# A two-layer diffusion backbone: summing the first MLP's second product in DRAM instead of in SBUF

## The chip, the cores and the metric

The kernel runs on one core of one Trainium2 chip. The metric is the device time of one execution in microseconds, and the number compared is the median of several runs. Three runs of the kernel before gave 1179.66, 1181.38 and 1181.9 us.

The engines are named as the profile names them: PE is TensorE (PEld its weight loads), DVE is VectorE, ACT is ScalarE, POOL is GpSimd and SP is SyncE, which in this kernel issues the transfers. PSUM is the memory into which matmuls accumulate, SBUF the working memory, DRAM the memory outside the core.

## What is computed

512 latent tokens and 256 context tokens, each a row of 1024 float32 numbers, go through two layers. Each layer mixes tokens (layer 0 by multi-scale pooling, layer 1 by attention) and then applies an MLP with a squared ReLU; every sub-layer is wrapped in RMS norms with shift, scale and gate from a conditioning vector. The part that matters here is the MLP of layer 0, which works on all 768 tokens:

```python
def sq_relu_mlp(h, w_in, w_out):                # h (768, 1024), w_in (1024, 4096), w_out (4096, 1024)
    return jnp.square(jax.nn.relu(h @ w_in)) @ w_out
...
m_lat = sq_relu_mlp(modulate(rms_norm(x, g_mlp_pre[i]), sh2, sc2), w_mlp_in[i], w_mlp_out[i])
x = x + gt2 * rms_norm(m_lat, g_mlp_post[i])
```

The second product, with w_out, is a sum over 4096 hidden columns. The kernel takes these in 16 groups of 256, so that the 768 x 1024 result is a sum over 16 groups.

## The kernel before, in words

**Numbers and tiles.** Every float32 operand of a matmul is split into a high and a low part (an ACT copy makes the high part, a DVE subtraction the low part), and a product is three matmuls: high x high, high x low, low x high. The 768 tokens are NT = 6 tiles of 128 rows. `acc` is a buffer of SBUF, [128, 6 x 1024] float32 (24 KB in each partition), and `accv[:, t]` is its tile t: 512 KB over the 128 partitions.

**The group loop** (`mlp0`, lines 798 to 824). For g = 0 to 14, one turn computes the hidden columns of group g + 1 (the "inner" product), and for g = 0 to 13 it also adds the second product of group g. For g = 0 the inner product is straightforward (class `Inner`); from g = 1 on it is done as seven smaller products by sums and differences of operands (class `Seven`, line 677), 12 matmuls each, 84 in all. After the fifth product DVE adds two results (lines 693 and 695) that the seventh product and the ReLU wait for. The second product (`out_mm`, line 757) takes, for each of the six tiles, two PSUM buffers of 128 x 512 from the pool `psB` (four buffers, shared with other uses) and 12 matmuls (line 773): 72 matmuls per group.

**Where the sum is kept.** `out_ev` (line 777) moves each PSUM buffer into `accv[:, t]`. In group 0 it copies (line 781, on ACT or DVE). In later groups there are two ways. The usual one is a DVE addition, acc = acc + PSUM (line 785). For tiles 1 and 4, in groups that `stale` doesn't exclude, the kernel "seeds": ACT first copies acc into the PSUM buffer (line 765), the matmuls accumulate onto it (start is false), and ACT copies the sum back (line 783). The last two groups, 14 and 15, are done together by `finish` (line 787) in tile order 4, 5, 0, 1, 2, 3: 24 matmuls per tile, then a DVE addition onto acc, and the norm and residual of that tile follow.

**Weights.** Per turn SP loads 1 MB of w_mlp_out, 1 MB of w_mlp_in and, until the list runs out, two pieces of 1 MB of w_ada, into the pool `rawp`, which has three buffers: a load can be issued when the buffer of three loads earlier has been read for the last time. The weights of w_mlp_out are split by ACT (line 126) and DVE (line 129). Those of w_mlp_in go through `weights_sums` (lines 635 to 665), with ACT casts at 643 and 659 and DVE operations at 644, 651 to 656 and 660. The pieces of w_ada are for `ada_sum` (lines 257 to 273), in which DVE multiplies and adds eight blocks (lines 263 and 268), transposes (271) and reduces (272). POOL has no work in this loop; it computes small row statistics (lines 161 to 169) elsewhere.

**What sets the order.** The kernel is written with a tile framework whose scheduler orders the instructions of each engine ahead of time, by its own model of durations, and places the semaphore waits; each engine then runs its list in order. In some places a list of due times (`Steps`) or a pinned order steers it. A transfer waits on the engine that issues it. `spill` is a tensor in DRAM that holds the residual rows (xr) during the MLP; they are read back (line 1158) ahead of the finish.

Of the kernel before, what the change touches and what calls it, by code (L numbers as in the profile page):

```python
# [9 lines left out]
F32 = mybir.dt.float32  # L10
# [3 lines left out]
ALU = mybir.AluOpType  # L14
# [3 lines left out]
P = 128  # L18
D = 1024
# [5 lines left out]
NT = TOK // P  # L25
# [28 lines left out]
def backbone(ctx: ExitStack, tc, x, c, ctx_in, c_ctx, w_ada, b_ada, g_mix_pre, g_mix_post,  # L54
# [3 lines left out]
    sy, ve, sc, gp, te = nc.sync, nc.vector, nc.scalar, nc.gpsimd, nc.tensor  # L58
# [14 lines left out]
    xr, gate, junk = residents(held[0])  # L73
    psA = ctx.enter_context(tc.tile_pool(name="psA", bufs=2, space=PSUM))
    psB = ctx.enter_context(tc.tile_pool(name="psB", bufs=4, space=PSUM))
    spill = ctx.enter_context(tc.tile_pool(name="spill", bufs=1, space=bass.MemoryType.DRAM)).tile([P, NT, D], F32, name="spill")

    acc = const.tile([P, NT * D], F32, name="acc")
    ident = const.tile([P, P], F32, name="ident")
    cols = const.tile([P, 128], F32, name="cols")  # L80
# [22 lines left out]
    accv = acc.rearrange("p (t n) -> p t n", n=D)  # L103
# [107 lines left out]
    ve.tensor_copy(cols, pp[:, 0:128])  # L211
    ve.tensor_copy(gpc, pp[:, 128:160])

    rowsd, parts, seeded, stale = {}, {}, {}, [0]

    def ada_mm(i, m, j, w=2):
        src = w_ada[i, :, m * D + j * 256: m * D + j * 256 + w * P].rearrange("(k p) n -> p k n", p=P)
# [23 lines left out]
    def ada_out(i, m, j, ps, nc_, w=2):  # L241
        at = m * KT + 2 * j
        ve.tensor_tensor(out=mods[i][:, at:at + w, 0:nc_], in0=ps.rearrange("p (b c) -> p b c", c=nc_),
                         in1=cols[:, i * 48 + at: i * 48 + at + w].unsqueeze(2).broadcast_to([P, w, nc_]),
                         op=ALU.add)
        if (i, m) == (0, SH1):
            ve.tensor_scalar(out=minus[:, 2 * j:2 * j + w], in0=mods[i][:, at:at + w, 0:nc_], scalar1=-1.0,
                             scalar2=None, op0=ALU.mult)
        if m in (SC1, SC2):
            s = 0 if m == SC1 else 1  # L250
            g0 = 96 + s * 16 + i * KT + 2 * j
            ve.scalar_tensor_tensor(out=avec[i][s][:, 2 * j:2 * j + w, 0:nc_], in0=mods[i][:, at:at + w, 0:nc_],
                                    scalar=1.0,
                                    in1=cols[:, g0:g0 + w].unsqueeze(2).broadcast_to([P, w, nc_]),
                                    op0=ALU.add, op1=ALU.mult)
# [19 lines left out]
    def ada_fin(i, m, parts, nc_):  # L275
        n = 4 * nc_
        ps = psB.tile([P, 512], F32, tag="b", name="psada")
        stale[0] = 4
        for a in range(4):
            te.matmul(ps[32 * a:32 * a + 32, 0:2 * n], sel,  # L280
                      parts.rearrange("p (u c b a) -> p a u b c", c=nc_, b=2, a=4)[:, a], start=True, stop=True)
        ada_out(i, m, 0, ps[:, 0:2 * n], nc_, 8)
# [314 lines left out]
    def spill_rows():  # L597
        for t in range(NT):
            tc.keep_in_program_order(sy.dma_start(spill[:, t], xr[:, t]))

    def sums():
        held[0].close()
        S["held"] = ExitStack()
        pool = S["held"].enter_context(tc.tile_pool(name="sums", bufs=1, side="right"))
        f, parts[0] = pool.tile([P, 8520], F32R, name="sums"), pool.tile([P, 192], F32, name="parts")
        u = unit[0]
        n4 = 4 * HN
        at = {1: (f[:, 0:n4], f[:, n4:2 * n4]), 2: (f[:, 2 * n4:3 * n4], f[:, 3 * n4:4 * n4]),
              4: (u[:, 0:n4], u[:, n4:2 * n4])}
        k4 = lambda z: [z[:, HN * k:HN * k + HN] for k in range(z.shape[-1] // HN)]  # L610
        for n, (hi, lo) in at.items():
            S[n] = k4(hi), k4(lo)
        h3, l3 = f[:, 4 * n4:5 * n4], [u[:, 2 * n4:2 * n4 + 2 * HN], f[:, 5 * n4:5 * n4 + 2 * HN]]
        S[3] = k4(h3), [z for x in l3 for z in k4(x)]
        src = acc.rearrange("p (q h u k n) -> p u h k q n", u=2, k=4, h=2, n=P)

        def put(n, j, a, b, op):
            hs = slice(2 * HN * j, 2 * HN * j + 2 * HN)
            wide = lambda z: z.rearrange("p (k q n) -> p k q n", k=2, n=P)
            w = work_tile()[:, 0:2 * HN]  # L620
            for m in range(2):
                ve.tensor_tensor(out=wide(w)[:, m], in0=a[:, m], in1=b[:, m], op=op)
            hi, lo = (h3[:, hs], l3[j]) if n == 3 else (z[:, hs] for z in at[n])
            sc.copy(hi, w)
            ve.tensor_tensor(out=lo, in0=w, in1=hi, op=ALU.subtract)
            return wide(w)

        for j in range(2):
            a11, a21, a12, a22 = (src[:, u, h, 2 * j:2 * j + 2] for u in range(2) for h in range(2))
            w1 = put(1, j, a21, a22, ALU.add)  # L630
            w2 = put(2, j, w1, a11, ALU.subtract)
            put(4, j, a12, w2, ALU.subtract)
            put(3, j, a11, a21, ALU.subtract)
# [73 lines left out]
    def w_in(i, g, rg, pin=False, wait=None):  # L707
        return rg.load(w_mlp_in[i, :, g * 256:(g + 1) * 256].rearrange("(k p) n -> p k n", p=P), 256, pin, wait)

    def w_out(i, g, rg, pin=False):  # L710
        return rg.load(w_mlp_out[i, g * 256:(g + 1) * 256, :].rearrange("(k p) n -> p k n", p=P), D, pin)
# [23 lines left out]
    order = (4, 5, 0, 1, 2, 3)  # L735
# [21 lines left out]
    def out_mm(i, parts, t, cols=HALVES):  # L757
        at_ = place_of[t] if i == 0 else t
        ts_ = slice(at_ * P, (at_ + 1) * P)
        seeded[t] = i == 0 and parts[0][0] > 0 and len(parts) == 1 and t in (1, 4) and stale[0] <= 0  # L760
        stale[0] -= 2
        pss = [psB.tile([P, 512], F32, tag="b", name="pso") for _ in cols]
        if seeded[t]:
            for (c0, w), ps in zip(cols, pss):
                sc.copy(ps, accv[:, t, c0:c0 + w])
        seq = [(a, f, w) for (_, (hi, lo), (wH, wL)) in parts for f in range(2)
               for a, w in ((hi, wH), (hi, wL), (lo, wH))]
        order = [(n, h) for n in range(len(seq)) for h in range(len(cols))]
        if len(parts) > 1:
            order.sort(key=lambda z: (z[0] >= (9 if cols == HALVES else 0), z[1]))  # L770
        for n, h in order:
            a, f, w = seq[n]
            te.matmul(pss[h][:, 0:cols[h][1]], a[:, f, ts_], w[:, f, cols[h][0]:sum(cols[h])],  # L773
                      start=(n == 0 and not seeded[t]), stop=(n == len(seq) - 1), skip_group_check=seeded[t])
        pso[t] = pss

    def out_ev(i, parts, t, cols=HALVES):
        for (c0, w), ps in zip(cols, pso[t]):
            d = accv[:, t, c0:c0 + w]
            if parts[0][0] == 0:  # L780
                (ve.tensor_copy if c0 and t % 3 else sc.copy)(d, ps)
            elif seeded[t]:
                sc.copy(d, ps)  # L783
            else:
                ve.tensor_tensor(out=d, in0=d, in1=ps[:, 0:w], op=ALU.add)  # L785

    def finish(i, parts, order, last, also=()):
        st = Steps()
        for z in also:
            st.at(*z)  # L790
        for n, t in enumerate(order):
            cols = THIRDS if (i, t) == (1, NL - 1) else HALVES
            st.at(5.2 * n, out_mm, i, parts, t, cols)
            st.at(5.2 * n + 5.2, out_ev, i, parts, t, cols)
            last(st, n, t)
        st.run()

    def mlp0(inner, hids, order, extra, mid, last, before_last):
        aH, aL = inner.a
        one = lambda z: Ring([z], True)  # L800
        wi = w_in(0, 1, one(unit[1]), True)
        spill_rows()
        for f in range(2):
            inner.square(f)
        wo_ = w_out(0, 0, one(unit[2]))
        sums()
        for g in range(NG - 1):
            if g:
                wo_, products = w_out(0, g, one(unit[2])), weights_sums(g + 1)
            part = (g, inner.hid, wo_)  # L810
            extra(g)
            if g:
                inner = Seven(products, hids[(g + 1) % len(hids)])
            else:
                inner = Inner(g + 1, wi, aH, aL, hids[(g + 1) % len(hids)], chunks0, TOK)
            inner.run((lambda: mid(g)) if g < NG - 2 else None)
            if g == NG - 2:
                wo_ = w_out(0, NG - 1, one(unit[1]))
            else:
                for t in range(NT):  # L820
                    out_mm(0, [part], t)
                    out_ev(0, [part], t)
        before_last()
        finish(0, [part, (NG - 1, inner.hid, wo_)], order, last)

# [504 lines left out]
    def last1(st, n, t):  # L1330
# [3 lines left out]
        st.at(5.2 * n + 7.8, fin_b, t)  # L1334

    mlp0(first[0], hids0, (4, 5, 0, 1, 2, 3), extra0, mid0, last0, before0)
    mlp1(first1[0], last1)

# [53 lines left out]
```

## Time and profile before

| | |
|---|---|
| median of three runs | 1181.38 us |
| runs | 1179.66 to 1181.9 us |
| span of the profiled execution, first to last instruction | 1177.7 us |
| median of the runs less that span | 3.7 us |
| moved by DMA | 147.84 MB, mean 126 GB/s |
| SP's queue (q1), share of 16 DMA engines over the span | 36.6% |
| mean granted TensorE clock | 0.994 |

The profiled execution's time is known by its span alone; a run's time holds about 3.7 us more than that. In the rows of the profile, "L773" is line 773 of the kernel before; `out<-in` names the tiles written and read; "x1152" is a count; the numbers after it are busy time in microseconds and the mean duration of one instruction in nanoseconds, then the idle time of the engine ahead of these instructions and what ended it. A row of a table of stretches gives the stretch, its length, and the busy time of each engine with its number of instructions. A row of transfers gives the count, the size of one and the median time from issue to landing in microseconds.

### The profile page before, as it was taken

What the parts mean: (1) busy time and instruction counts of PE and PEld (TensorE: products, weight loads), DVE (VectorE), ACT (ScalarE), POOL (GpSimd) and SP (SyncE); (2) the same over time, 40 slices, a digit from 0 to 9 for tenths busy, and PEclk for the clock granted to TensorE, in tenths of its full rate; (3) what the DMA queues carried; (4) which work ended last, traced back from release to release, by engine and by line L of the source; (5) the groups of instructions that cost most, each with busy time, mean ns of one, the idle gap of its engine ahead of it and who ended that gap; (6) DMA issues with size and microseconds to landing.
All of it is one profiled execution on the core that took longest, in us unless ns stands there. A gap on an engine that the chain in (4) does not pass through costs nothing.

```text
span 1177.7 us, 15984 instructions
## 1 busy us (share of the span) xinstructions
PE 1142.0 (97%) x6170; PEld 988.8 (84%) x6170; DVE 941.6 (80%) x1546; ACT 638.0 (54%) x1087; POOL 67.4 (6%) x120
## 2 busy tenths in 40 slices
PE   5899999999999999999999999999899999999997
PEld 4579888989889988998887889998888888888886
DVE  3786778998988999896787689887686779778876
ACT  3766654555354445555676377862676446435522
POOL 2030000000000000000141210001100000000001
PEclk9899999999999999999999999999999999999999
DMA  9994223444444344344422100115334124314312
GB/s 335 353 310 183 72 72 107 143 143 144 143 143 143 116 136 143 107 133 153 180 72 77 68 1 36 37 42 186 122 116 162 67 94 143 107 36 144 107 39 104
DMA packets 100010, 147.84 MB, mean 126 GB/s; under 512 B 2736, under 2 KB 75872, under 8 KB 99936
## 3 DMA queue, kind: packets, MB, share of 16 engines
q1 hardware_dynamic: 99936, 146.84, 36.6%
q8 instruction: 48, 0.79, 0.3%
q14 instruction: 26, 0.21, 0.1%
HBM read 139.49 MB, written 7.34 MB: 125 GB/s over the span
## 4 chain that ended last, share of the span: by engine, by line
PE 52%; issue 33%; DVE 6%; ACT 4%; POOL 3%; DMA 2%; SPq 0%; POOLq 0%; DVEq 0%; ACTq 0%
PE pso L773 22%; PE psin L677 18%; PE psin L553 3%; PE po L1234 2%; PE psq L1020 2%; PE pss L1195 2%; POOL rs L169 1%; PE psada L225 1%; PE psm L420 1%; POOL rs L1029 1%; ACT junk L154 1%; DVE sm L1199 1%; PE pspt L1220 1%; DVE rows L268 1%; DVE units L1223 1%
## 5 line engine op out<-in xcount | busy, mean ns | idle before, releaser
L773 PE MATMUL pso<-units,rb 128*128 128x512 f32 x1152 | 278.9, 392 | 0.0
L773 PEld LDWEIGHTS pso<-units,rb 128*128 128x128 f32 x1152 | 214.7, 188 | 41.1
L268 DVE SCALAR_TENSOR_TENSOR rows<-raw,cond,rows 128x256 f32<-128x256 f32 x280 | 127.3, 480 | 2.0
L785 DVE TENSOR_TENSOR acc<-acc,pso 128x512 f32<-128x512 f32 x129 | 85.4, 677 | 39.4 <-PE pso L773 39.3
L553 PE MATMUL psin<-ra,rb 128*128 128x512 f32 (+1 forms) x432 | 104.8, 342 | 2.4 <-ACT ra L363 1.6
L877 PE MATMUL pso<-units,pairs 128*128 128x512 f32 x336 | 82.3, 389 | 0.0
L553 PEld LDWEIGHTS psin<-ra,rb 128*128 128x128 f32 x432 | 70.3, 189 | 13.6 <-ACT ra L363 1.9
L553 PE MATMUL psin<-ra 128*128 128x512 f32 x256 | 80.4, 389 | 0.0
L877 PEld LDWEIGHTS pso<-units,pairs 128*128 128x128 f32 x336 | 63.1, 188 | 13.1
L881 DVE TENSOR_TENSOR acc<-acc,pso 128x512 f32<-128x512 f32 x72 | 48.7, 683 | 26.4 <-PE pso L877 26.4
L167 POOL TENSOR_SCALAR ms<-ss 128x1 f32<-128x1 f32 x20 | 9.6, 482 | 1000.2 <-ACT junk L154 988.4
L677 PE MATMUL psin<-ra,units 128*128 128x384 f32 x336 | 65.5, 337 | 0.4 <-ACT psin L689 0.4
L677 PE MATMUL psin<-sums,units 128*128 128x384 f32 x336 | 64.0, 336 | 0.0
L677 PEld LDWEIGHTS psin<-ra,units 128*128 128x128 f32 x336 | 59.8, 188 | 3.9 <-ACT psin L689 0.5
L129 DVE TENSOR_TENSOR units<-raw,units 128x1024 fp32r<-128x1024 f32 (+2 forms) x49 | 55.2, 1154 | 6.5 <-ACT units L126 6.3
L677 PEld LDWEIGHTS psin<-sums,units 128*128 128x128 f32 x336 | 58.9, 188 | 1.6
L126 ACT CAST units<-raw 128x1024 fp32r<-128x1024 f32 (+2 forms) x49 | 46.9, 995 | 17.7 <-PE pso L773 13.7
L553 PEld LDWEIGHTS psin<-ra 128*128 128x128 f32 x256 | 48.1, 188 | 10.0
L553 PE MATMUL psin<-rb 128*128 128x512 f32 (+1 forms) x144 | 52.8, 367 | 0.2 <-DVE rb L364 0.2
L1020 PE MATMUL psq<-units,ra 128*128 128x512 f32 x216 | 51.7, 392 | 0.0
L783 ACT COPY acc<-pso 128x512 f32<-128x512 f32 x48 | 27.1, 586 | 43.6 <-PE pso L773 42.9
L553 PE MATMUL psin<-rb,ra 128*128 128x512 f32 x128 | 49.8, 389 | 0.0
(255 smaller groups left out, 2356.0 us busy)
## 6 DMA issues: line engine op xcount, KB each, us to landing
raw<-in_w_ada SPq DMA_DIRECT2D x48, 1024.0 KB, 5.4
raw<-in_w_mlp_in SPq DMA_DIRECT2D x32, 1024.0 KB, 5.4
raw<-in_w_mlp_out SPq DMA_DIRECT2D x32, 1024.0 KB, 5.1
raw<-in_w_qkv SPq DMA_DIRECT2D x6, 1024.0 KB, 5.2
spill<-xr SPq DMA_DIRECT2D x10, 512.0 KB, 9.1
xr<-spill SPq DMA_DIRECT2D x10, 512.0 KB, 6.6
raw<-in_w_o SPq DMA_DIRECT2D x4, 1024.0 KB, 4.9
xr<-in_x SPq DMA_DIRECT2D x4, 512.0 KB, 4.2
```

The lines of the kernel that those rows point to most:

```text
L126: a = sc.copy(hi, raw)
L129: b = ve.tensor_tensor(out=lo, in0=raw, in1=hi, op=ALU.subtract)
L268: ve.scalar_tensor_tensor(out=r, in0=raw[:, k, :], scalar=cond[:, k, c:c + 1], in1=r, op0=ALU.mult, op1=ALU.add)
L553: te.matmul(ps[:, bank, o:o + ln], w[:, k, fs], rhs, start=start, stop=(k == KT - 1 and n == 2), skip_group_check=len(ks) < KT)
L677: te.matmul(bank, w[k], a[k], start=start and k == 0 and m == 0, stop=stop and k == 3 and m == 2, skip_group_check=True)
L773: te.matmul(pss[h][:, 0:cols[h][1]], a[:, f, ts_], w[:, f, cols[h][0]:sum(cols[h])], start=(n == 0 and not seeded[t]), stop=(n == len(seq) ...
L783: sc.copy(d, ps)
L785: ve.tensor_tensor(out=d, in0=d, in1=ps[:, 0:w], op=ALU.add)
L877: te.matmul(ps, a, w, start=(m == 0), stop=(m == len(seq) - 1))
L881: ve.tensor_tensor(out=M[n][:, t], in0=M[n][:, t], in1=ps, op=ALU.add)
L1020: te.matmul(ps, a[:, k, sl], w[:, k % 4, :], start=(k == 0 and n == 0), stop=(k == KT - 1 and n == 2))
L1195: te.matmul(ps[:, c2, 0:384], a[:, sl], b[:, kv, 384 * c2:384 * c2 + 384], start=(n == 0), stop=(n == 2))
```

## The change

The second product of groups 0 to 13 is no longer summed in SBUF. ACT copies both PSUM buffers of a tile into `accv[:, t]`, which is now only a staging place, and POOL issues a transfer of that 512 KB tile to a new DRAM tensor `total`: in group 0 as a plain write, in groups 1 to 13 with `accum_op=add`, so that the transfer adds to what `total` holds. After the loop POOL issues six transfers that read `total` back into `accv`, and `finish` goes on as before. The seeding of tiles 1 and 4 and its bookkeeping are gone. There are 84 transfers into `total` and 6 out of it.

By the framework's waits, each adding transfer waits for the transfer of the same tile one group earlier to have landed; the first copy into a tile of `accv` waits for that tile's transfer of the group before; each read-back waits for that tile's last addition.

```diff
-    spill = ctx.enter_context(tc.tile_pool(name="spill", bufs=1, space=bass.MemoryType.DRAM)).tile([P, NT, D], F32, name="spill")
+    spill = ctx.enter_context(tc.tile_pool(name="spill", bufs=1, space=bass.MemoryType.DRAM))
+    total = spill.tile([P, NT, D], F32, name="total")
+    spill = spill.tile([P, NT, D], F32, name="spill")
...
     def out_mm(i, parts, t, cols=HALVES):
-        seeded[t] = i == 0 and parts[0][0] > 0 and len(parts) == 1 and t in (1, 4) and stale[0] <= 0
-        stale[0] -= 2
         pss = [psB.tile([P, 512], F32, tag="b", name="pso") for _ in cols]
-        if seeded[t]:
-            for (c0, w), ps in zip(cols, pss):
-                sc.copy(ps, accv[:, t, c0:c0 + w])
...
-                      start=(n == 0 and not seeded[t]), stop=(n == len(seq) - 1), skip_group_check=seeded[t])
+                      start=(n == 0), stop=(n == len(seq) - 1))
...
     def out_ev(i, parts, t, cols=HALVES):
         for (c0, w), ps in zip(cols, pso[t]):
             d = accv[:, t, c0:c0 + w]
-            if parts[0][0] == 0:
-                (ve.tensor_copy if c0 and t % 3 else sc.copy)(d, ps)
-            elif seeded[t]:
+            if i == 0 and len(parts) == 1:
                 sc.copy(d, ps)
             else:
                 ve.tensor_tensor(out=d, in0=d, in1=ps[:, 0:w], op=ALU.add)
+        if i == 0 and len(parts) == 1:
+            how = dict(accum_op=ALU.add) if parts[0][0] else {}
+            gp.dma_start(total[:, t], accv[:, t], **how)
...
                 for t in range(NT):
                     out_mm(0, [part], t)
                     out_ev(0, [part], t)
+        for t in order:
+            gp.dma_start(accv[:, t], total[:, t])
         before_last()
         finish(0, [part, (NG - 1, inner.hid, wo_)], order, last)
```

The changed lines shift the numbering: lines of the changed kernel are 1 to 2 higher up to line 300 or so (L129 becomes L131, L263 L265, L272 L274), 1 higher from there to line 760 (L643 becomes L644, L651 L652, L693 L694), the matmul at L773 is L769, the copy of the eviction L777, the transfer L782 and the read-back L821. SP issues the same loads in the same order.

More of the change, by code (lines that the diff above doesn't have):

```diff
@@ L212, in backbone @@
     ve.tensor_copy(gpc, pp[:, 128:160])
-    rowsd, parts, seeded, stale = {}, {}, {}, [0]
+    rowsd, parts = {}, {}
     def ada_mm(i, m, j, w=2):
@@ L277, in ada_fin @@
         ps = psB.tile([P, 512], F32, tag="b", name="psada")
-        stale[0] = 4
         for a in range(4):
```

## The prediction

> **What bounds the kernel now.** I read the totals first.
>
> ```profile
> span 1177.7 us, 15984 instructions
> PE 1142.0 (97%) x6170; PEld 988.8 (84%) x6170; DVE 941.6 (80%) x1546; ACT 638.0 (54%) x1087; POOL 67.4 (6%) x120
> ```
>
> PE is busy 97% of the span. A busy PE need not be a PE at its rate, so I then took the stretches of the first MLP: its whole group loop, and two stretches from one group's seventh product to the next group's.
>
> ```profile
> 256.60:287.80 31.20, 31.20 (x158) 28.16 (x157) 28.16 (x52) 15.55 (x24) 0.00 (x0) 1.00 0.44 145
> 227.70:256.60 28.90, 28.90 (x148) 26.26 (x146) 27.16 (x52) 14.44 (x23) 0.00 (x0) 1.00 0.41 135
> 125.50:555.00 429.50, 429.50 (x2172) 385.67 (x2171) 371.10 (x673) 218.66 (x326) 0.00 (x0) 1.00 0.38 125
> ```
>
> The columns are stretch, length, then busy time of PE, PEld, DVE, ACT, POOL, the clock, the DMA share and GB/s. Over 429.5 us PE is never idle and the clock is 1.00. The groups of matmuls in the two stretches say whether it also runs at its rate:
>
> ```profile
> L773 PE MATMUL pso<-units,rb 128*128 128x512 f32 x73 | 17.9, 392 | 0.0
> ...
> L773 PE MATMUL pso<-units,rb 128*128 128x512 f32 x63 | 15.6, 392 | 0.0
> ```
>
> The first row is of the 31.2 us stretch, the second of the 28.9 us one; both hold the 84 matmuls of seven products. Ten matmuls more cost 2.3 us, 0.23 us each, which is the mean busy time of one inside each row (17.9/73 and 15.6/63, 0.25). So the stage's time is its number of matmuls; nothing in it waits for DVE or ACT. A full group is 72 matmuls into pso and those 84, 31.2 us. What the other engines may lose in a group before PE notices is DVE 3.0 us (31.2 - 28.2), ACT 15.6, POOL all, DMA 56%.
>
> **The change, part by part.** What is evicted, by operation, within the group loop (rows of tile pso):
>
> ```profile
> L785 DVE TENSOR_TENSOR acc<-acc,pso x108: 646/683/693, 153.0 to 553.2; 128x512 f32<-128x512 f32 x108
> L765 ACT COPY pso<-acc x48: 572/582/602, 147.4 to 541.1; 128x512 f32<-128x512 f32 x48
> L783 ACT COPY acc<-pso x48: 567/588/593, 153.9 to 548.7; 128x512 f32<-128x512 f32 x48
> L781 ACT COPY acc<-pso x8: 577/588/592, 128.6 to 145.9; 128x512 f32<-128x512 f32 x8
> L781 DVE COPY acc<-pso x4: 682/689/692, 131.3 to 147.0; 128x512 f32<-128x512 f32 x4
> ```
>
> *DVE* loses 108 x 0.683 + 4 x 0.689 = 76.5 us, 5.5 per group (of 14). *ACT* loses 48 x 0.582 + 56 x 0.588 = 60.9 us and gains 168 x 0.588 = 98.8: 2.7 us more per group, 18.3 of 31.2. *PE* does the same matmuls; only start flags differ. With PE at its rate, the relief of DVE buys nothing: the gain term is 0, at most the one idle time of PE just behind the loop, 0.43 us:
>
> ```profile
> 556.88 2.37 PE L677 MATMUL psin<-ra,units 128*128 128x384 f32 x12 [0.43 <-ACT psin L689]
> ```
>
> *POOL and DMA* get 84 transfers of 512 KB into DRAM, 78 of them adding, and 6 reading back. The stage now moves this:
>
> ```profile
> raw<-in_w_ada SPq DMA_DIRECT2D x24, 1024.0 KB, 5.3
> raw<-in_w_mlp_out SPq DMA_DIRECT2D x14, 1024.0 KB, 5.2
> raw<-in_w_mlp_in SPq DMA_DIRECT2D x13, 1024.0 KB, 5.3
> ```
>
> Four loads of 1 MB per group, 5.3 us from issue to landing. The engine time of one load, and the rate of full engines while rows of xr are read back from DRAM:
>
> ```profile
> 107.80:112.80 5.00, 5.00 (x34) 5.00 (x33) 2.59 (x6) 4.89 (x9) 0.00 (x0) 1.00 0.66 210
> 566.00:570.00 4.00, 4.00 (x21) 3.44 (x20) 2.40 (x4) 3.82 (x6) 0.00 (x0) 1.00 1.05 414
> ```
>
> A load alone takes 0.66 x 5 = 3.3 us of all 16 engines. At 414 GB/s a plain 512 KB transfer takes 1.27 us. An adding transfer is not in this trace. Its lower end is the plain copy, 1.27; the upper end is the landing time of a store to DRAM, if each had the engines to itself:
>
> ```profile
> spill<-xr SPq DMA_DIRECT2D x10, 512.0 KB, 9.1
> xr<-spill SPq DMA_DIRECT2D x10, 512.0 KB, 6.6
> ```
>
> That is 9.1 us, far. I take 2.6, near the copy row: each adding transfer must read 512 KB twice, from SBUF and from DRAM, and write once, so twice the copy. The Trainium skill ("Collectives: The Full Stack", the section on the bandwidth ceiling) says that an add in the DMA engines halves their rate because it needs two source reads, with a measured ratio of 1.93; no row here shows it, and by it the price would be an estimated 2.5 us and the sum below 2 us less.
>
> Engine time per group: 4 x 3.3 + 6 x 2.6 = 28.8 of 31.2 us. It fits, barely. While a load is under way, the adding transfers take half of the engines (2.6 of every 31.2/6 = 5.2 us), so its 3.3 us become 6.6: each load lands about 3.3 us later, or 5.2 later if it meets two of them. Evictions come in bursts, on the chain of work:
>
> ```profile
> 163.80 4.80 PE pso L773 x21
> ...
> 222.80 5.03 PE pso L773 x22
> ```
>
> A tile is 12 matmuls, so a burst ends nearly two tiles in 5 us, and two transfers follow each other.
>
> *Who waits for a load?* In before, ACT already does:
>
> ```profile
> ACT units L643 <- DMA raw<-in_w_mlp_in: 17.8, 11, 6.3
> ...
> DVE rows L263 <- DMA raw<-in_w_ada: 4.0, 3, 2.1
> ```
>
> In the order of DVE's instructions there is a shift. Before, the two adds of the seven products (L693, L695) stood ahead of the first use of w_mlp_in (L651) in most groups; in the changed kernel that use (L652) stands ahead of them (L694, L696) in every group that has it. PE's seventh product waits for L694. So a late load now holds PE through DVE, and through ACT, where the evictions that free psB stand behind the cast that waits for it (L644).
>
> The load of w_mlp_in can start only when the ada_sum three loads earlier has let its buffer go. Between that and L652, DVE has in every second group the rest of one ada_sum, in the others the split of w_mlp_out, and the load of w_ada behind that split is exposed every second group too. From these rows (210 to 540 us):
>
> ```profile
> L268 DVE SCALAR_TENSOR_TENSOR rows<-raw,cond,rows 128x256 f32<-128x256 f32 x222 | 101.2, 480 | 1.4
> ...
> L129 DVE TENSOR_TENSOR units<-raw,units 128x1024 fp32r<-128x1024 f32 x21 | 25.1, 1218 | 0.0
> ...
> L271 DVE STREAM_TRANSPOSE raw<-rows 128x256 f32<-128x256 f32 x33 | 14.2, 438 | 0.2
> ...
> L272 DVE TENSOR_REDUCE parts<-raw 128x16 f32<-128x512 f32 (+1 forms) x22 | 12.1, 549 | 0.1
> ...
> L693 DVE TENSOR_TENSOR work<-work,psin 128x384 f32<-128x384 f32 x11 | 6.0, 549 | 6.7 <-PE psin L677 6.5
> ```
>
> First kind: 8 x 0.48 + 2 x 0.44 + 0.55 = 5.3 us, which just hides a load of 5.3. Second kind: 2 x 1.22 = 2.4, exposed 2.9. The w_ada load: 5 L268, 2.4, exposed 2.9. Per group: 1.45 + 1.45 = 2.9 us of exposed load from 1.5 loads. DVE's round is then 28.2 - 5.5 = 22.7 busy, + 2.9 exposed, + 0.6 waiting for PE at L693 = 26.2 us. Each exposed load that is 3.3 later makes it 26.2 + 5.0 = 31.2: exactly PE's time. 5.2 later makes it 26.2 + 7.8 = 34.0, 2.8 over. I take half of the groups as meeting two: 1.4 us per group, over the 13 groups whose transfers add, **+18 us**.
>
> *The end of the stage.* The last eviction starts at 553.2; the first add that needs the rows read back:
>
> ```profile
> L785 DVE TENSOR_TENSOR acc<-acc,pso x12: 675/678/689, 574.5 to 605.2; 128x512 f32<-128x512 f32 x12
> ```
>
> at 574.5, 21 us later. An adding transfer and a read-back one behind the other take 9.1 + 6.6 = 15.7 us at most by the two queued 512 KB rows above; hidden, cost 0. Were the cover gone, the cost is what exceeds 21 us. POOL's next work, the row statistics, stands behind the read-backs in its queue, and needs those rows anyway. The read-backs add 6 x 1.27 = 7.6 us of engine time near the six reloads of xr, which feed the residual adds and not PE's matmuls of the finish.
>
> Each adding transfer also waits for the one of the same rows a group earlier, and each eviction for that transfer to have read its rows: both 31 us old, free unless the queue is behind.
>
> Sum: 0 + 18 + 0 on the profiled span of 1177.7 gives 1195.7. The median of the runs, 1181.38, is 3.7 above the profiled span, so **1199 us**.
>
> **The rivals.** *Hidden (not slower).* Adding transfers spread evenly, each exposed load 3.3 later, DVE's round 31.2: PE still sets the time, 1177.7 + 3.7 = 1181. It decides at an extra of 3.3 us per load. For it: DVE's 5.5 us of relief; against it: the order on DVE, and two engines of equal round lose at every mismatch. Faster by more than 0.2% would need PE idle time to remove, and the stage has 0.4 us; only a shift in later stages could do it, whose order on PE is practically unchanged.
>
> *The adding transfers are the bound.* At three times the copy (3.8 us) the engines need 13.2 + 22.8 = 36 us a group, 4.8 over: 13 x 4.8 = 62, 1244. At the far end, 9.1: 13.2 + 54.6 = 67.8, 36.6 over, 476, 1657. For it: 28.8 of 31.2 leaves no room for an error in the 2.6.
>
> *POOL is late with issuing.* POOL instructions stretch beside DVE:
>
> ```profile
> 605.53 0.56 POOL L169 TENSOR_TENSOR rs<-ms,nhalf 128x1 f32<-128x1 f32 x1
> ...
> 612.21 2.67 POOL L169 TENSOR_TENSOR rs<-ms,nhalf 128x1 f32<-128x1 f32 x1
> ```
>
> the same operation by 2.1 us. From 5.2 us per issue on, POOL sets the stage; at 6, 13 x 6 x 0.8 = 62, also 1244. Against it: POOL has nothing else to do in the loop (0.00 busy), so it needs a stretch of several us on each issue. The Trainium skill ("SBUF — State Buffer", the section on two separate sides) has such a rule: while VectorE runs an operation that takes both ports, GpSimd can't write descriptors and its DMA stands still; no run here shows it yet.
>
> **How the numbers follow.** Forecast (loads late, part of it reaching PE): 0.38. Hidden: 0.27. Transfers the bound: 0.24. POOL the bound: 0.05. Faster by some shift elsewhere: 0.06. A difference under 0.2% (2.4 us) can't be told from none here. So faster 0.06, same 0.27, slower 0.67. The range starts at 1178, under the hidden case, and ends at 1290, at which an adding transfer costs 4.4 us (13 x 8.4 = 109 over); left out are the faster case and some 0.12 of dearer transfers.
>
> **What would show it.** Right: DMA share near 0.9 in the group loop; landings of the weight loads from 5.3 to 8 us or more; DVE at some 23 us a group, with longer waits at L652 and L265; PE idle of about a microsecond per group in front of the seventh product (L678 waiting for DVE) or of pso matmuls waiting for ACT; read-backs landed well before the first add of the finish. Wrong: PE idle 0 in the loop (hidden); or ACT's copies waiting for adding transfers, POOL's queue full and landings over 10 us (transfers or POOL the bound).

## The result, and the profile after

The changed kernel took 1235.88 us (median of four runs, 1230.06 to 1242.72) against 1180.52 us for the kernel before beside it: a ratio of 1.047 (95% interval 1.0445 to 1.0494), 55 us slower. The forecast was 1199. The profiled execution is the longest of the four: its time is 1242.72 us, its span 1240.9. Differences taken from its rows come out some 8 us above that of the medians. (A run's time is here 1.8 us above its own span. The 3.7 us ahead of the prediction compare a median with the span of one single execution.)

The totals of the changed kernel's page, and its group loop, in the columns of the table of stretches:

```profile
span 1240.9 us, 16218 instructions
PE 1163.4 (94%) x6170; PEld 1001.1 (81%) x6170; DVE 878.7 (71%) x1434; ACT 665.7 (54%) x1151; POOL 140.9 (11%) x210
```

```profile
237.80:565.40 327.60, 297.90 (x1437) 264.26 (x1436) 211.20 (x401) 158.88 (x252) 46.32 (x54) 0.95 0.84 202
```

The span grew by 63.2 us. PE executes the same 6170 matmuls but is busy for 21.4 us more, and idle for the other 41.8. The stretch is nine groups, from one group's first transfer after the long wait (237.76) to that of the ninth group later (565.43): 36.4 us per group where TensorE alone needs 31.2 (the full group of the kernel before). DVE and ACT are busy for less than before in each us, PE is idle for 9% of the stretch, and the DMA engines are busy for 0.84 of it.

The queues and the transfers of the changed kernel between 160 and 590 us (share of 16 engines; then count, size, median us from issue to landing):

```profile
q0 software_dynamic: 10401, 37.89, 50.4%
q1 hardware_dynamic: 39555, 49.18, 33.5%
...
total<-acc POOLq DMA_DIRECT2D x74, 512.0 KB, 6.5
raw<-in_w_ada SPq DMA_DIRECT2D x23, 1024.0 KB, 8.1
raw<-in_w_mlp_out SPq DMA_DIRECT2D x13, 1024.0 KB, 7.5
raw<-in_w_mlp_in SPq DMA_DIRECT2D x12, 1024.0 KB, 9.4
```

37.89 MB are 72.3 pieces of 512 KB, so an adding transfer holds all engines for 0.504 x 430 / 72.3 = 3.0 us, and six of them for 18 us per group. Every load lands later than the 5.2 to 5.3 us of before, w_mlp_in by 4.1 and w_ada by 2.8 us.

What DVE and PE wait for in the same nine groups (us in total, times, longest):

```profile
DVE work L652 <- DMA raw<-in_w_mlp_in: 92.5, 9, 17.4
DVE rows L265 <- DMA raw<-in_w_ada: 18.6, 9, 3.1
DVE work L694 <- PE psin L678: 2.3, 2, 1.2
DVE units L645 <- ACT units L644: 0.4, 1, 0.4
```

```profile
PE pso L769 <- ACT acc L777: 19.6, 6, 4.4
PE psin L678 <- ACT work L692: 9.7, 2, 5.0
PE psin L678 <- DVE work L694: 0.3, 1, 0.3
```

DVE's 211.2 us of work and its 111.1 us of waiting for loads fill the stretch but for 5 us. It waits for PE for 2.3 us in nine groups: it no longer follows PE, it sets the pace. PE in turn hardly ever waits for DVE; its idle time ends with ACT. One group's timeline of the changed kernel shows how the two fit together (start, duration; in brackets the idle time ahead and its end):

```profile
255.54 0.37 SPq L109 DMA_DIRECT2D raw<-in_w_mlp_out  x1
...
258.18 0.85 POOL L782 DMA_DIRECT2D total<-acc  x1 [7.75 <-ACT acc L777]
...
259.53 0.87 POOL L782 DMA_DIRECT2D total<-acc  x1 [0.50 <-ACT acc L777]
259.55 0.42 DVE L274 TENSOR_REDUCE parts<-raw 128x8 f32<-128x256 f32 x1
259.99 0.37 SPq L109 DMA_DIRECT2D raw<-in_w_mlp_in  x1
...
270.52 1.04 ACT L644 CAST units<-raw 128x1024 fp32r<-128x1024 f32 x1 [9.64 <-DMA raw<-in_w_mlp_in]
270.52 0.69 DVE L652 TENSOR_TENSOR work<-raw 128x512 f32<-128x512 f32 x1 [10.55 <-DMA raw<-in_w_mlp_in]
...
272.94 1.06 ACT L777 COPY acc<-pso 128x512 f32<-128x512 f32 x2
...
273.57 2.92 PE L769 MATMUL pso<-units,rb 128*128 128x512 f32 x6 [3.51 <-ACT acc L777]
```

The load of w_mlp_in goes out at 259.99, the moment the ada_sum that held its buffer has ended (L274). Issued in the eight microseconds ahead of it are a load of w_ada (at 251.78), the load of w_mlp_out and two adding transfers. As an estimate, with 3.3 us of engine time for a load, that is 3 x 3.3 + 2 x 3.0 = 15.9 us from 251.78 on, so 267.7 if all of them are served first; it is used at 270.52. In the 15 us before its use the DMA engines are busy for 0.96:

```profile
255.50:270.50 15.00, 14.56 (x73) 12.72 (x71) 4.18 (x10) 2.64 (x5) 1.72 (x2) 1.00 0.96 280
```

DVE and ACT both stand still for this load for ten microseconds. On ACT the evictions of finished tiles (L777) stand behind the cast that waits (L644), so the PSUM buffers stay full and PE stops.

### The profile page after: what moved, and what is told of

It is laid out like the page before. It is cut to its first block, busy times and chain, and to the rows that moved or that the text cites. A ratio compares the mean times of both kernels' runs of the same rounds, so it can differ in the third digit from the quotient of the medians.

```text
span 1240.9 us, 16218 instructions
## 1 busy us (share of the span) xinstructions
PE 1163.4 (94%) x6170; PEld 1001.1 (81%) x6170; DVE 878.7 (71%) x1434; ACT 665.7 (54%) x1151; POOL 140.9 (11%) x210
## 5 line engine op out<-in xcount | busy, mean ns | idle before, releaser
L769 PE MATMUL pso<-units,rb 128*128 128x512 f32 x1152 | 285.1, 399 | 26.7 <-ACT acc L777 25.7
L769 PEld LDWEIGHTS pso<-units,rb 128*128 128x128 f32 x1152 | 217.1, 191 | 74.0 <-ACT acc L777 29.3
L270 DVE SCALAR_TENSOR_TENSOR rows<-raw,cond,rows 128x256 f32<-128x256 f32 x280 | 122.3, 479 | 2.7
L782 POOL DMA_DIRECT2D total<-acc x84 | 70.6, 843 | 432.3 <-ACT acc L777 431.0
L777 ACT COPY acc<-pso 128x512 f32<-128x512 f32 x168 | 91.1, 587 | 27.0 <-PE pso L769 26.4
L652 DVE TENSOR_TENSOR work<-raw 128x512 f32<-128x512 f32 x14 | 9.7, 692 | 126.2 <-DMA raw<-in_w_mlp_in 126.2
L644 ACT CAST units<-raw 128x1024 fp32r<-128x1024 f32 x14 | 14.7, 1047 | 111.2 <-DMA raw<-in_w_mlp_in 108.4
L169 POOL TENSOR_SCALAR ms<-ss 128x1 f32<-128x1 f32 x20 | 11.5, 577 | 519.3 <-ACT junk L156 507.5
L880 DVE TENSOR_TENSOR acc<-acc,pso 128x512 f32<-128x512 f32 x72 | 48.8, 683 | 27.6 <-PE pso L876 27.6
L131 DVE TENSOR_TENSOR units<-raw,units 128x1024 fp32r<-128x1024 f32 (+2 forms) x49 | 55.7, 1153 | 13.7 <-ACT units L128 13.5
```

Source lines behind the costliest of these rows:

```text
L131: b = ve.tensor_tensor(out=lo, in0=raw, in1=hi, op=ALU.subtract)
L270: ve.scalar_tensor_tensor(out=r, in0=raw[:, k, :], scalar=cond[:, k, c:c + 1], in1=r, op0=ALU.mult, op1=ALU.add)
L644: sc.copy(k4(hi), src)
L782: gp.dma_start(total[:, t], accv[:, t], **how)
L880: ve.tensor_tensor(out=M[n][:, t], in0=M[n][:, t], in1=ps, op=ALU.add)
```

## The experiments

Theory A is that of late loads: the adding transfers hold the DMA engines, and with three buffers taken in turn the landings of w_mlp_in and w_ada lie in one chain with DVE's work. Its rivals: the move of all evictions to ACT costs by itself (B); the adding transfer as such, its issue or its number, costs; the engines' time is simply full. Each time below stands against the kernel before in the same series (1180.04, then 1180.25, then 1179.48 us).

**No adding transfers.**

```diff
-        if i == 0 and len(parts) == 1:
+        if i == 0 and len(parts) == 1 and not parts[0][0]:
             how = dict(accum_op=ALU.add) if parts[0][0] else {}
```

> This kernel leaves out the adding transfers of groups 1 to 13, so the sum over the groups; evictions stay plain copies on ScalarE as in the changed kernel. Theory A (late weight loads: the adding transfers hold the DMA engines, the loads land at 8 to 9.4 us instead of 5.3, and three raw buffers put two landings of each group into one chain with VectorE's work): without transfers 1178 to 1185 us, landings 5.3 us, TensorE never idle in the loop, clock 0.99. Theory B (the move of all evictions to ScalarE, which runs in order, costs by itself): 1225 to 1236 us. If relief of VectorE by 5.5 us per group is worth anything, this kernel is faster than before: under 1178.

1180.72 us, ratio 1.0003 (0.9992 to 1.0015). B falls: evictions on ACT and the new order cost nothing. And the relief of DVE earns nothing, so what the change could have gained at best is 0. Its DVE waits over nine groups (240 to 520.8 us):

```profile
DVE work L652 <- DMA raw<-in_w_mlp_in: 45.8, 9, 7.9
DVE units L645 <- ACT units L644: 9.2, 4, 4.3
DVE work L694 <- PE psin L678: 8.7, 4, 3.8
DVE rows L265 <- DMA raw<-in_w_ada: 3.5, 4, 1.0
```

Even without a single adding transfer, DVE waits for w_mlp_in for 5 us per group on the mean (0.87 us in two of the nine groups, 5.4 to 7.9 in the other seven). The same wait in the kernel before:

```profile
DVE work L651 <- DMA raw<-in_w_mlp_in: 2.2, 5, 1.0
```

That is 2.2 us in all. The difference lies in what DVE has to do between the issue of the load and its first use. One group of the kernel before, then one of the run without adding transfers:

```profile
252.98 0.37 SPq L107 DMA_DIRECT2D raw<-in_w_mlp_in  x1
...
253.85 1.67 DVE L268 SCALAR_TENSOR_TENSOR rows<-raw,cond,rows 128x256 f32<-128x256 f32 x4
255.44 0.69 DVE L785 TENSOR_TENSOR acc<-acc,pso 128x512 f32<-128x512 f32 x1
...
259.09 0.69 DVE L651 TENSOR_TENSOR work<-raw 128x512 f32<-128x512 f32 x1
```

```profile
246.73 0.37 SPq L109 DMA_DIRECT2D raw<-in_w_mlp_in  x1
...
254.16 0.69 DVE L652 TENSOR_TENSOR work<-raw 128x512 f32<-128x512 f32 x1 [7.46 <-DMA raw<-in_w_mlp_in]
```

In the kernel before, six microseconds of work cover the load. Only 1.4 us of them are additions of the sum (two of L785); the rest is mainly the next ada_sum (L268) and the add at L695. In the new order that other work stands behind L652. In two of the nine groups a whole ada_sum is still left between issue and use, in the other seven nothing. PE doesn't notice: it is the slower of the two here, but not by much (DVE's work and its waits for loads are 258.8 of the 280.8 us).

**Plain writes.**

```diff
-            how = dict(accum_op=ALU.add) if parts[0][0] else {}
+            how = {}
```

> The transfers stay, as many and as large, but write instead of add (it leaves out the sum). Engine time of six per group 6 x 1.27 = 7.6 us instead of 18. Theory A: landings of w_mlp_in about 6.5 to 7.5 us, of which most fits in the slack of the chain (about 2.6 us per group before): 1181 to 1195 us. If the number or the bytes of the transfers cost, not the adding: 1220 or more. Theory B: 1236.

1184.06 us, ratio 1.0031 (1.0017 to 1.0044): as A has it. Queue q0 between 160 and 550 us (77 writes and the first read-backs):

```profile
q0 software_dynamic: 11209, 40.86, 27.3%
```

40.86 MB are 77.9 pieces of 512 KB, so 0.273 x 390 / 77.9 = 1.37 us of engine time each, where an adding one takes 3.0: 2.2 times as much. (The 1.33 in the expectation for two plain writes comes from counting 80 pieces.)

**Narrow transfers**, still adding and as many.

```diff
+            n = 64 if parts[0][0] else D
-            gp.dma_start(total[:, t], accv[:, t], **how)
+            gp.dma_start(total[:, t, 0:n], accv[:, t, 0:n], **how)
```

> The changed kernel with as many adding transfers, each of 64 columns of 1024 instead of all (it leaves out most of the sum): same issues on GpSimd, same waits, a sixteenth of the bytes. If bytes that are added hold the engines: 1179 to 1186 us and landings of the loads near 5.5 us. If what costs is the adding transfer as such (a fixed price, the issue of 0.85 us, GpSimd's queue): 1215 to 1236.

1180.01 us, ratio 0.9999 (0.9988 to 1.001). The same 84 issues, waits and read-backs cost nothing; it is the size of the transfers. (A sixteenth of the bytes is not a sixteenth of the engine time: q0 still has 11.5% of the engines between 160 and 550 us, against 50.5% in the changed kernel.)

**Two plain writes for each adding transfer** (`second` is another tensor in DRAM).

```diff
-            how = dict(accum_op=ALU.add) if parts[0][0] else {}
-            gp.dma_start(total[:, t], accv[:, t], **how)
+            for z in (total, second):
+                gp.dma_start(z[:, t], accv[:, t])
```

> Every adding transfer is replaced by two plain writes of the same 512 KB into two DRAM tiles (it leaves out the sum). A plain write took 1.33 us of engine time in the run with plain writes, so a group's transfers take 12 x 1.33 = 16 us, nearly the 18 of six adding ones, with twice the issues at 0.54 us. If it is engine time that counts, whatever the kind: between four adding transfers (12 us, +29 us) and six (18 us, +55 us): 1215 to 1238. If the adding itself (the read of DRAM ahead of the write, conflicts there) is what delays the loads: 1184 to 1200.

1213.72 us, ratio 1.0298 (1.0259 to 1.0338), a microsecond under the range, far from the rival's. Its queue between 160 and 550 us:

```profile
q0 software_dynamic: 20448, 74.46, 50.1%
```

74.46 MB are 142 pieces, 1.38 us each, so 16.5 us per group. Nothing adds here, and the kernel loses 34 us all the same: engine time counts, whatever it is spent on.

**Two of six tiles, and four of six, through DRAM**, in the kernel before, whose other tiles stay as they were (the lines that make `total` and read it back are left out of the diff; for four tiles `VIA` is (0, 2, 3, 5)).

```diff
-    pso = {}
+    pso, VIA = {}, (0, 3)
...
-            if parts[0][0] == 0:
+            if i == 0 and len(parts) == 1 and t in VIA:
+                sc.copy(d, ps)
+            elif parts[0][0] == 0:
...
+        if i == 0 and len(parts) == 1 and t in VIA:
+            how = dict(accum_op=ALU.add) if parts[0][0] else {}
+            gp.dma_start(total[:, t], accv[:, t], **how)
```

> The kernel before, where only tiles 0 and 3 of the six go by adding transfers and the other four keep their evictions (seeds of tiles 1 and 4 included). Two adding transfers per group are 2 x 3.0 = 6 us of engine time beside 13.2 of loads. Chain theory (a group is as long as the longer of TensorE's 31.2 us and the chain of two landings and VectorE's work, with some us of slack): the landings grow by about a third of what six did, inside the slack: 1180 to 1190 us. If the loss goes linearly with the transfers: 1181 + 55 x 2/6 = 1199.

> As the run with two, with tiles 0, 2, 3 and 5 by adding transfers and the two others as before. 12 us of engine time beside 13.2. Chain theory: landings grow by two thirds of what six did (w_mlp_in about 8, w_ada about 7 us), slack used up: 1190 to 1212 us, less than two thirds of the loss (1217) and more than twice the loss with two. Linear: 1217.

1184.7 us, ratio 1.0039 (1.0023 to 1.0054), and 1209.46 us, ratio 1.0247 (1.0227 to 1.0267). Not linear: the first two tiles cost 4.5 us, the next two 25, the last two 26. Some 6 to 8 us of engine time per group find room, and then each further transfer costs 12 to 13 us. The kernels in one table (engine time of the group's transfers into DRAM; for two, four and six at 3.0 us each). The order is right, but they aren't points of one curve: with two and four, the other tiles keep their evictions of before.

| transfers per group | engine time, us | loss, us |
|---|---|---|
| none | 0 | +0.7 |
| two adding | 6 | +4.5 |
| six plain | 8 | +4.0 |
| four adding | 12 | +29 |
| twelve plain (two per tile) | 16.5 | +34 |
| six adding | 18 | +55 |

**Contention with the evictions of before.**

```diff
+        if i == 0 and len(parts) == 1:
+            how = dict(accum_op=ALU.add) if parts[0][0] and True else {}
+            gp.tensor_copy(sm_tile("sm")[:, 0:8], accv[:, t, D - 8:D])
+            gp.dma_start(total[:, t], S['f'][:, 0:D], **how)
```

(`S['f']` is the tile of sums, which stays unchanged in the loop; nothing is read back. The lines that make `total` and keep `S['f']` are left out.)

> The kernel before, with its evictions as they were, and beside them the same number of adding transfers of 512 KB, each from a resident tile and behind a small mark on GpSimd that follows the tile's eviction; nothing is read back. Theory A: contention alone brings the loss, and VectorE's 5.5 us more per group stand in the same chain: 1236 to 1300 us, landings 8 to 10 us. Theory B: the evictions are those of before, so 1181 to 1190 us.

1292.26 us, ratio 1.0943 (1.092 to 1.0965). The transfers (with a small mark on POOL each), beside DVE's additions as they were, cost 112 us, so contention alone is enough for a loss. As a size this doesn't carry over: the first transfer waited 35 us for the tile of sums, and those behind it then ran as a backlog, which the changed kernel has not:

```profile
POOL total L792 <- ACT sums L627: 35.3, 1, 35.3
```

Queue and loads of this kernel between 200 and 380 us:

```profile
q0 software_dynamic: 8037, 29.25, 82.0%
...
raw<-in_w_mlp_in SPq DMA_DIRECT2D x3, 1024.0 KB, 33.4
```

Here the price of an adding transfer comes out lower: 29.25 MB are 55.8 pieces, 0.82 x 180 / 55.8 = 2.6 us each. In this backlog POOL issues one about every 2.9 to 3.0 us (298.38, 301.30, 304.29), with loads between them. So 3.0 is the price in the changed kernel, and not a constant.

**Raw buffers of their own.** The changed kernel with whole transfers; in the loop each of the three kinds of load keeps one of the three buffers.

```diff
+    fixed = {}
-    def raw_load(src, width, pool=None):
-        t = (pool or pools[0]).tile([P, 2048], F32, tag="raw", name="raw")
+    def raw_load(src, width, pool=None, own=None):
+        if own is not None:
+            t = fixed[own] = fixed.get(own) or rawp.tile([P, 2048], F32, tag="raw", name="raw")
+        else:
+            t = (pool or pools[0]).tile([P, 2048], F32, tag="raw", name="raw")
```

> The changed kernel, where in the loop the loads of w_mlp_out, w_mlp_in and w_ada each keep one raw buffer of their own instead of taking the three in turn, so that w_mlp_in is issued when its own last use is over, not when the last w_ada sum is. Theory A with the chain of buffers: landings stay 8 to 10 us but lie further ahead of their use: 1188 to 1212 us. If the DMA engines' time itself is the bound (6 x 3.0 + 4 x 3.3 = 31.2 us per group of 31.2): 1230 to 1240, and the DMA share rises little. Theory B: 1236.

1191.68 us, ratio 1.0091 (1.0066 to 1.0116). Of 55 us, 44 are gone with the same transfers. (The calls that pass `own`, one name for each kind of load, are left out of the diff.) Two controls followed, the same buffers in the kernel before and with narrow transfers:

> Control: the kernel before, with one raw buffer each for w_mlp_out, w_mlp_in and w_ada in the loop, no transfers. TensorE bounds the loop before, so nothing should come of it: 1176 to 1185 us. If it were faster by several us, the run with separate buffers would have gained from something other than the landings; if it is slower, part of that run's remaining 11 us belongs to the buffers.

> The changed kernel with separate raw buffers and adding transfers of 64 columns only (it leaves out most of the sum). Separate buffers cost the kernel before 20 us, at the end of the loop. If the 11 us that the run with separate buffers and whole transfers still lacks come from the buffers: 1188 to 1196. If they come from the transfers: 1178 to 1184.

The kernel before took 1199.92 us with them, ratio 1.0166 (1.0151 to 1.0181): a miss. Its loop keeps its pace (PE busy for 427.8 of 430 us), and just behind it PE waits for the last of the ada sums:

```profile
PE psada L285 <- DVE parts L277: 11.2, 2, 10.9
```

Where the rest of its 20 us comes from was not followed up.

In the changed kernel, whose DVE has less to do, the buffers cost little: with narrow transfers 1182.79 us, ratio 1.0026 (1.0015 to 1.0037). Of the 11.6 us that the run with whole transfers still lacks, some 8 belong to the transfers and 3 to the buffers.

**Only w_mlp_in with a buffer of its own**, the two others in turn.

```diff
+            if own != "in":
+                turn[0] += 1
+                own = turn[0] % 2
```

> The changed kernel with whole adding transfers; only w_mlp_in keeps a raw buffer of its own, w_mlp_out and w_ada take two in turn. If the late landing of w_mlp_in is the main thing (VectorE and ScalarE both stand for it for 10.6 us): 1185 to 1205. If the two landings of w_ada in a chain with VectorE count as much: 1212 to 1236.

1189.56 us, ratio 1.008 (1.0052 to 1.0109). Its stretch from 160 to 550 us, its queues there, and what DVE waits for:

```profile
160.00:550.00 390.00, 387.80 (x1951) 348.40 (x1950) 283.45 (x533) 218.90 (x345) 64.46 (x76) 1.00 0.97 233
```

```profile
q0 software_dynamic: 11014, 40.14, 58.1%
q1 hardware_dynamic: 40704, 50.33, 38.7%
...
raw<-in_w_ada SPq DMA_DIRECT2D x24, 1024.0 KB, 9.2
raw<-in_w_mlp_in SPq DMA_DIRECT2D x12, 1024.0 KB, 7.6
```

```profile
DVE rows L273 <- DMA raw<-in_w_ada: 78.6, 12, 7.9
...
DVE work L702 <- PE psin L686: 14.6, 9, 3.8
```

The engines are busier than in the changed kernel (0.97), w_ada lands later, and yet PE is idle for only 2.2 us of 390 and its clock is 1.00 (it gets through 1951 matmuls there, 1975 in the kernel before). No row of DVE or ACT waits for w_mlp_in any more: it is issued 15 us ahead of its first use, and that use now waits for PE:

```profile
203.48 0.37 SPq L117 DMA_DIRECT2D raw<-in_w_mlp_in  x1
```

```profile
218.51 1.05 ACT L652 CAST units<-raw 128x1024 fp32r<-128x1024 f32 x1 [1.03 <-PE psin L686]
```

So full DMA engines as such are not the bound. Some 45 of the 55 us that the changed kernel lost, it lost because w_mlp_in can't be asked for until the last ada_sum (in some groups the split of w_mlp_out) has let its buffer go. The order on each engine shifts a little with the buffers, too. With a buffer for each kind of load and narrow transfers (1182.79) that earned nothing; for the buffers of this run there is no such control. The last 10 us stay with the transfers and buffers, and were not taken apart.

None of these kernels is faster than the one before, and the run without adding transfers says why: with the whole sum left out, the time is still that of before, so there was nothing to gain by moving it.

## Why the prediction was wrong

**PE bounds the loop, the relief of DVE is worth 0: right.** Shown by the run without adding transfers.

**An adding transfer takes 2.6 us of engine time: right in kind, low by 0.4.** It is 3.0 in the changed kernel, 2.2 plain writes (and 2.6 in the backlog of the contention kernel). The Trainium skill ("Collectives: The Full Stack", the section on the bandwidth ceiling) has 1.93 for the ratio of its AllGather to its ReduceScatter. The changed kernel is above it, the backlog near it (2.6 / 1.37 = 1.9); the rows decide. Engine time per group was then 13.2 + 18 = 31.2 us, not 28.8.

**Loads land 3.3 or 5.2 us later: about right.** 4.1 for w_mlp_in, 2.8 for w_ada, of which some tenths for w_mlp_in come without any adding transfer (6.0 us instead of 5.3 in the nine groups of the run without them). DVE waited for loads 12.3 us per group (111.1 / 9), against 5.5 without adding transfers (49.3 / 9): 6.8 us more, between the 5.0 and the 7.8 of the prediction.

**"Per group: 1.45 + 1.45 = 2.9 us of exposed load from 1.5 loads. DVE's round is then 28.2 - 5.5 = 22.7 busy, + 2.9 exposed, + 0.6 waiting for PE": this is the step that failed.** The mechanism was right, this term was mis-sized. Without adding transfers the exposed load is 5.5 us, nearly twice the 2.9: 5.1 for w_mlp_in and 0.4 for w_ada. The prediction had an ada_sum cover w_mlp_in in every second group, and the split of w_mlp_out a part of it in the others. In the nine groups shown an ada_sum covers it in two, and in seven nothing does: the split covers it in none, and in two of them it is the split that lets the buffer go (it ends at 335.13 us, the load goes out at 335.15). It also gave the load 5.3 us from issue to landing, but it goes out behind w_mlp_out and was used 5.4 to 7.9 us after its issue. For w_ada it was the other way round: 0.4 us, not 1.45. DVE's round in the changed kernel is 211.2 / 9 = 23.5 busy + 12.3 = 35.8 us, and 36.4 with the rest, not 31.2 or 34.0.

**"I take half of the groups as meeting two: 1.4 us per group": fell with it.** With a base of 26.2 a lateness of 5.0 just fits under 31.2, and only half of the groups lose. With the base as measured, every one of the nine groups shown is over (33.2 to 38.9 us each), by 5.2 us on the mean: 2.6 from the exposed loads (5.5 - 2.9), 1.8 from the lateness (6.8 - 5.0), 0.8 from DVE's work (23.5 - 22.7). That is 46.8 us; the remaining groups and the end of the stage have the other 16 of the span's 63.

**How PE is held: the second of the two ways that the prediction gave.** It put DVE's L694 first; that row is 0.3 us. PE waits for evictions on ACT behind the cast of w_mlp_in (19.6 us of the nine groups) and for ACT's L692 (9.7).

**The read-back is hidden, POOL is in time: right in the loop, and nearly so at its end.** DVE waits for a read-back once, for 2.8 us:

```profile
L779 DVE TENSOR_TENSOR acc<-acc,pso 128x512 f32<-128x512 f32 x3 | 2.1, 688 | 6.5 <-PE pso L769 3.6 <-DMA acc<-total 2.8
```

POOL's idle time in front of its transfers ends with ACT, and an issue takes 0.84 us, not the 5.2 from which POOL would set the stage:

```profile
L782 POOL DMA_DIRECT2D total<-acc x84 | 70.6, 843 | 432.3 <-ACT acc L777 431.0 <-issue 0.6
```

Behind the loop the read-backs stand in POOL's queue between the last additions, and three of them wait for a transfer to land (16.8 us in all). The last four additions are issued late by that, from 600.5 to 622.2 us; the 2.8 us above are the only wait of DVE that shows there.

**The rival with the transfers as the bound** had 1244 for 3.8 us each. That this is near the measured time is luck: at the measured 3.0 us its own sum is 31.2 of 31.2 us, no loss, and the run with a buffer of its own for w_mlp_in has the same transfers and 1189.56. That makes the lateness, not the fullness, the main cause.

## What to carry to other kernels

When work is taken off an engine that is not the bound, its order changes as well, and waits for loads that other work covered can come into view: the engine's round then shrinks by less than the work. Before adding up a round, list for several groups of the changed order what stands between each load's issue and its use; and where extra transfers are to run beside loads, first look whether each load is issued well ahead of its use, or only when the buffer of another, unrelated user comes free. Here that one buffer was worth some 45 of 55 us.

## What the runs showed of the hardware

The granted clock falls after a short stop. Stretches of the changed kernel around the stall of 3.51 us that ends at 273.57:

```profile
258.00:262.30 4.30, 4.30 (x27) 4.26 (x26) 1.83 (x4) 1.57 (x3) 1.72 (x2) 1.00 1.08 348
273.50:276.30 2.80, 2.73 (x7) 2.15 (x8) 2.77 (x6) 0.91 (x3) 0.86 (x1) 0.50 0.27 23
276.30:279.90 3.60, 3.60 (x14) 3.57 (x13) 3.60 (x11) 3.49 (x7) 0.85 (x1) 0.61 0.71 127
280.00:284.00 4.00, 4.00 (x20) 3.30 (x19) 4.00 (x9) 3.69 (x6) 0.85 (x1) 1.00 0.99 144
```

From 1.00 to 0.50, and back to 1.00 about 6.5 us later. The Trainium skill ("TensorE: Matmul & The Clock Gate", the part on the clock gate) says that the clock halves after an idle window of about 3.4 us; this stall agrees. PE's 21.4 us more of busy time for the same matmuls are mostly of this kind (the clock of the nine groups is 0.95, which is an estimated 0.05 x 297.9 = 15 us of them; with a buffer of its own for w_mlp_in it is 1.00). They were not in the prediction, but they hardly add to the loss: DVE set the pace in these groups and waited for PE for 2.3 us in nine. They show that busy time of PE is not work done.

An adding transfer also costs POOL more to issue than a plain one: 0.84 us on the mean of 84 (78 of them adding), against 0.54 in the run with two plain writes.

```profile
L783 POOL DMA_DIRECT2D total<-acc x84 | 45.5, 542 | 389.3 <-ACT acc L778 388.4
```
